# GpSimd's low parts of weight pieces, written in two operations of half the rows instead of one

## The chip, the cores and the metric

The kernel runs on one core of one Trainium2 chip. The core has five engines with a queue of instructions each: TensorE (PE in the profile, with its weight loads as PEld), VectorE (DVE), ScalarE (ACT), GpSimd (POOL) and SyncE (SP), which here only issues DMAs. Every queue is worked off in its order, and an instruction waits for semaphores that other engines raise. The metric is the device time of one execution in microseconds (us), shorter is better.

## What is computed

Two layers of a token backbone over 256 latent tokens and 256 context tokens of width 1024. A layer is a normalised and modulated input, one wide input projection, three mixing branches (latent attention, a long convolution, differential attention), their merge by sigmoid gates, an output projection, and a squared-ReLU MLP of width 4096. Cut to what matters here, the large products with weights:

```python
p  = h @ w_in                              # 1024 -> 5024, latent and context tokens
m  = g_a*(ya @ w_br_a) + g_b*(yb @ w_br_b) + g_c*(yc @ w_br_c)
y  = m @ w_out
x  = x + g_m * y
x  = x + g_f * (square(relu(h2 @ w_fc1)) @ w_fc2)   # 1024 -> 4096 -> 1024
```

All of it is float32. In the second layer only the 256 latent tokens go on after the attention's keys and values.

## The kernel before

**Weights in two parts.** TensorE multiplies float32 data in a format of fewer bits, fp32r. To keep the accuracy, each operand is split into a high part (the value cast to fp32r) and a low part (the value minus its high part), and `mm3` (line 265) makes each product of three matmuls: high by high (L270), low activations by high weights (L271 where the weight stands first) and high activations by low weights (L272). The profile's names tell which is which: `whi` and `wlo` are the parts of the weight, `hhi` and `hlo` those of the activations.

**Pieces.** A weight arrives from HBM in blocks of 1 MB (`raw`, two buffers), and a block is cut into pieces (`Unit`) of 128 partitions by 1024 values. Of a piece, the cast to `whi` runs on ScalarE in most cases (L222), and then the subtraction that makes `wlo` runs on VectorE (157 pieces of L223) or on GpSimd (69 pieces of L223, 3 of L234 in `split_rows` and 2 of L245 in `split_into`: 74 in all). `whi` and `wlo` have three buffers each. A piece is split one piece ahead of its use (`LOOK`).

**Which engine.** `pick_lo` (line 209) takes GpSimd or VectorE for the low part by a default that the caller sets (`lo_eng`) and by single exceptions in the table `CHOICE`. A piece is 8 rows of 128 values (`split_cols`, `split_into`) or 4 rows of 256 (`split_rows`) on each partition; a row k is what one group of three matmuls uses, so TensorE comes to a piece's rows one after the other.

**Order.** The steps are lists of Python functions that are woven by hand and then put in an order by the table `ORDER`; each engine's queue holds its instructions in the order in which the steps were written. The framework adds the waits: an instruction waits for the last writer of what it reads and for the last readers of what it overwrites.

**What stands around the GpSimd pieces.** VectorE has, beside its own low parts, the softmax of the attentions (`DVE L799` maximum out of PSUM, `L1226` and `L1230` which combine two probability tiles), the rotary step (`L787`, `L790`), the low parts of activations (`L480`, `L497`, `L277`), the merge (`L1324`, `L1328`) and parts of the MLP's squaring (`L1428`, `L1429`). GpSimd has also rotary products (`L789`), copies (`L1171`) and a few others. The wait of a new block's DMA (`SPq L254`) is for the last reader of the old block in that buffer, which is often a GpSimd low part.

Of the kernel before, what the change touches and what calls it, by code (L numbers as in the profile page):

```python
# [9 lines left out]
F32 = mybir.dt.float32  # L10
F32R = mybir.dt.float32r
AF = mybir.ActivationFunctionType
ALU = mybir.AluOpType
# [110 lines left out]
def backbone_kernel(ctx: ExitStack, tc: tile.TileContext, t, out):  # L124
# [9 lines left out]
    PE, ACT, DVE, POOL, SP = nc.tensor, nc.scalar, nc.vector, nc.gpsimd, nc.sync  # L134
# [64 lines left out]
    def pick(key, default):  # L199
        return CHOICE.get(key, default)  # L200
# [4 lines left out]
    def cp(key, default="A"):  # L205

        return {"A": ACT.copy, "D": DVE.tensor_copy, "P": POOL.tensor_copy}[pick(key, default)]

    def pick_lo(u, eng):
        return ENG[pick(f"lo{u.id}", "P" if eng is POOL else "D")]  # L210

    def split_cols(lo_col, own=None):
        eng = lo_eng["e"]

        def f(raw, u):
            if own:
                u.hi, u.lo = [S[own].tile([128, KT, 128], F32R, name=f"{own}{p}{lo_col}") for p in "hl"]
            else:
                u.hi = ring.tile([128, KT, 128], F32R, tag="whi", name="whi", bufs=UNIT_BUFS)
                u.lo = ring.tile([128, KT, 128], F32R, tag="wlo", name="wlo", bufs=UNIT_BUFS)  # L220
            src = raw[:, :, lo_col:lo_col + 128]
            cp(f"hi{u.id}")(u.hi, src)  # L222
            pick_lo(u, eng).tensor_tensor(out=u.lo, in0=src, in1=u.hi.bitcast(F32), op=ALU.subtract)  # L223
        return f

    def split_rows(kt0):
        eng = lo_eng["e"]

        def f(raw, u):
            u.hi = ring.tile([128, 4, 256], F32R, tag="whi", name="whi", bufs=UNIT_BUFS)  # L230
            u.lo = ring.tile([128, 4, 256], F32R, tag="wlo", name="wlo", bufs=UNIT_BUFS)
            src = raw[:, kt0:kt0 + 4, :]
            cp(f"hi{u.id}")(u.hi, src)
            pick_lo(u, eng).tensor_tensor(out=u.lo, in0=src, in1=u.hi.bitcast(F32), op=ALU.subtract)  # L234
        return f

    def split_into(lo_col, keep, c0):

        eng = lo_eng["e"]

        def f(raw, u):
            u.hi, u.lo = [b[:, :, c0:c0 + 128] for b in keep()]
            src = raw[:, :, lo_col:lo_col + 128]
            cp(f"hi{u.id}")(u.hi, src)
            pick_lo(u, eng).tensor_tensor(out=u.lo, in0=src, in1=u.hi.bitcast(F32), op=ALU.subtract)  # L245
        return f

    def rawtile(shape):
# [9 lines left out]
    def gemm_units(blk):  # L258
        return [Unit(blk, split_cols(0)), Unit(blk, split_cols(128))]
# [592 lines left out]
    def mla(l, nt):  # L852
# [5 lines left out]
        uq_ = w_in_units(l, 0)  # L858
        b2 = col_blk(t["w_in"][l], 0, C_PKV, 192)
        ukv_ = [Unit(b2, split_cols(c, "kvw" if l else None)) for c in (0, 64)]  # L860

        def g_pq(i):
# [286 lines left out]
    def diff(l, nt):  # L1149
# [25 lines left out]
        for which, c0 in ((0, C_DQ), (1, C_DK)):  # L1175
            qks.append([Step(qk(which, ct), Unit(col_blk(t["w_in"][l], 0, c0 + 128 * ct, 128), split_cols(0)))
                        for ct in range(2)])
# [492 lines left out]
```

## Time and profile before

| | |
|---|---|
| three runs, median (lowest to highest) | 1349.06 us (1346.07 to 1350.47) |
| the profiled execution, its own time | 1347.23 us |
| its span, first to last instruction | 1345.2 us |
| mean granted clock of TensorE | 0.984 |
| busy: TensorE, weight loads | 1289.5 us (96%), 1082.9 us (81%) |
| busy: VectorE, ScalarE, GpSimd | 876.7 us (65%), 588.0 us (44%), 257.6 us (19%) |
| the chain that ended last: TensorE, VectorE, ScalarE, GpSimd | 81%, 10%, 3%, 0% |

The profiled execution is 2.0 us longer than its span, and 1.8 us shorter than the median. The rows of a timeline read: start in us, length in us, engine, line, operation, what it writes and reads, how many were merged, and in brackets how long the engine was idle before and who ended that. A line of the waits reads: who waited for whom, total us, times, longest. A matmul's length includes its pipeline; how fast TensorE goes is seen in the distance between starts.

### The profile page before, as it was taken

How to read it: one execution, taken by the hardware profiler on the slowest of the kernel's cores; microseconds unless marked ns; L12 is line 12 of the kernel's file. 1: busy time of each engine (PE TensorE's matmuls, PEld its weight loads, DVE VectorE, ACT ScalarE, POOL GpSimd, SP SyncE). 2: the span in 40 equal slices, each digit the busy share in tenths (PEclk: the TensorE clock that was granted, in tenths of full speed). 3: DMA queues.
4: the chain of work that ended last, by engine and by line, in shares of the span. 5: the costliest groups of instructions: out<-in, count | busy, mean ns of one | idle time of the engine just before them, and what ended most of it. 6: DMA issues, size and time to landing. Idle time of an engine off the chain costs nothing.

```text
span 1345.2 us, 19813 instructions
## 1 busy us (share of the span) xinstructions
PE 1289.5 (96%) x7934; PEld 1082.9 (81%) x7934; DVE 876.7 (65%) x1406; ACT 588.0 (44%) x1034; POOL 257.6 (19%) x173
## 2 busy tenths in 40 slices
PE   4999999899999999999999999998998999999997
PEld 3576776567888898787787877996887999999997
DVE  4776736865244568986684775587667568976565
ACT  4454542564222344332332332364646654655343
POOL 2212131310001101120100112022234343230100
PEclk8899999999999999999999999998999999999999
DMA  9643243442233334654564553332133455455652
GB/s 267 176 147 112 79 125 105 148 152 70 91 102 98 109 100 128 216 188 162 168 200 128 170 160 115 111 103 78 49 97 99 127 164 162 157 188 183 191 186 94
DMA packets 159789, 185.20 MB, mean 138 GB/s; under 512 B 4880, under 2 KB 149233, under 8 KB 157650
## 3 DMA queue, kind: packets, MB, share of 16 engines
q1 hardware_dynamic: 158162, 182.27, 43.2%
q0 software_dynamic: 928, 1.54, 0.4%
q8 instruction: 62, 1.02, 0.3%
q14 instruction: 29, 0.24, 0.1%
q10 hardware_dynamic: 608, 0.14, 0.0%
HBM read 182.88 MB, written 1.05 MB: 137 GB/s over the span
## 4 chain that ended last, share of the span: by engine, by line
PE 81%; DVE 10%; ACT 3%; DMA 2%; issue 2%; POOL 0%; SPq 0%; ACTq 0%; DVEq 0%; POOLq 0%
PE g L270 15%; PE g L271 15%; PE g L272 14%; PE s L270 9%; PE s L272 9%; PE s L271 9%; PE o L839 2%; PE t L826 2%; PE mod L338 1%; DVE d L1168 1%; DVE hlo L480 1%; DVE wlo L223 1%; DMA mq<-in_w_mod_dram 1%; ACT whi L222 1%; ACT t L156 1%
## 5 line engine op out<-in xcount | busy, mean ns | idle before, releaser
L222 ACT CAST whi<-raw 128x1024 fp32r<-128x1024 f32 x203 | 212.7, 1049 | 443.3 <-PE g L271 215.7
L270 PE MATMUL g<-hhi,whi 128*128 128x512 f32 (+2 forms) x1040 | 355.3, 342 | 5.5 <-ACT ge L1297 1.6
L272 PE MATMUL g<-hhi,wlo 128*128 128x512 f32 (+2 forms) x1040 | 353.4, 340 | 0.5 <-DVE wlo L223 0.5
L271 PE MATMUL g<-hlo,whi 128*128 128x512 f32 (+2 forms) x1040 | 353.2, 340 | 0.2
L223 POOL TENSOR_TENSOR wlo<-raw,whi 128x1024 fp32r<-128x1024 f32 x69 | 174.2, 2526 | 637.5 <-ACT whi L222 503.8
L223 DVE TENSOR_TENSOR wlo<-raw,whi 128x1024 fp32r<-128x1024 f32 x157 | 194.2, 1238 | 146.2 <-ACT whi L222 138.7
L270 PEld LDWEIGHTS g<-hhi,whi 128*128 128x128 f32 x1040 | 196.4, 189 | 37.5 <-issue 7.0
L271 PEld LDWEIGHTS g<-hlo,whi 128*128 128x128 f32 x1040 | 197.0, 189 | 23.5 <-issue 0.8
L272 PEld LDWEIGHTS g<-hhi,wlo 128*128 128x128 f32 x1040 | 197.1, 190 | 23.2 <-DVE wlo L223 0.9
L374 DVE SCALAR_TENSOR_TENSOR macc<-modr,spad,macc 128x1024 f32<-128x1024 f32 x84 | 112.2, 1365 | 16.0 <-DMA modr<-in_w_mod_dram 15.0
L1350 DVE SCALAR_TENSOR_TENSOR x<-s,modT,x 128x256 f32<-128x256 f32 x95 | 43.4, 480 | 72.6 <-PE s L272 72.5
L272 PE MATMUL s<-hid0h,wlo 128*128 128x512 f32 (+1 forms) x256 | 87.0, 340 | 0.0
L271 PE MATMUL s<-hid0l,whi 128*128 128x512 f32 (+1 forms) x256 | 86.7, 339 | 0.0
L270 PE MATMUL s<-hid0h,whi 128*128 128x512 f32 (+1 forms) x256 | 86.6, 338 | 0.0
L272 PE MATMUL s<-hid1h,wlo 128*128 128x256 f32 (+1 forms) x224 | 72.7, 325 | 0.0
L270 PE MATMUL s<-hid1h,whi 128*128 128x256 f32 (+1 forms) x224 | 72.6, 324 | 0.0
L271 PE MATMUL s<-hid1l,whi 128*128 128x256 f32 (+1 forms) x224 | 72.2, 323 | 0.0
L156 ACT ACTIVATE t<-s,sm 128x512 f32<-128x512 f32 (+1 forms) x91 | 55.4, 612 | 36.6 <-DVE sm L799 35.9
L799 DVE TENSOR_REDUCE sm<-s 128x1 f32<-128x512 f32 (+1 forms) x75 | 51.4, 688 | 26.5 <-PE s L272 19.5
L270 PEld LDWEIGHTS s<-hid0h,whi 128*128 128x128 f32 x256 | 48.4, 189 | 7.3 <-ACT whi L222 0.8
L271 PEld LDWEIGHTS s<-hid0l,whi 128*128 128x128 f32 x256 | 48.0, 187 | 5.8
L272 PEld LDWEIGHTS s<-hid0h,wlo 128*128 128x128 f32 x256 | 48.1, 188 | 5.7
(467 smaller groups left out, 2433.7 us busy)
## 6 DMA issues: line engine op xcount, KB each, us to landing
raw<-in_w_fc_dram SPq DMA_DIRECT2D x64, 1024.0 KB, 5.4
raw<-in_w_in_dram SPq DMA_DIRECT2D x34, 1024.0 KB, 5.3
modr<-in_w_mod_dram SPq DMA_DIRECT2D x48, 512.0 KB, 4.3
raw<-in_w_mod_dram SPq DMA_DIRECT2D x16, 1024.0 KB, 5.0
mq<-in_w_mod_dram SPq DMA_DIRECT2D x16, 512.0 KB, 7.9
raw<-in_w_out_dram SPq DMA_DIRECT2D x8, 1024.0 KB, 5.1
raw<-in_w_in_dram SPq DMA_DIRECT2D x8, 512.0 KB, 3.9
raw<-in_w_br_a_dram SPq DMA_DIRECT2D x8, 512.0 KB, 3.4
```

The lines of the kernel that those rows point to most:

```text
L156: ins = ACT.activation(out=out, in_=in_, func=func, **kw).ins
L222: cp(f"hi{u.id}")(u.hi, src)
L223: pick_lo(u, eng).tensor_tensor(out=u.lo, in0=src, in1=u.hi.bitcast(F32), op=ALU.subtract)
L270: PE.matmul(ps, lhsT=ah, rhs=bh, start=first and i == 0, stop=False)
L271: PE.matmul(ps, lhsT=ah, rhs=bl, start=False, stop=False)
L272: PE.matmul(ps, lhsT=al, rhs=bh, start=False, stop=last and i == n - 1)
L338: PE.matmul(box["ps"][32 * j:32 * j + 32, :], lhsT=spad[:, kt, :], rhs=raw[:, 512 * j:512 * (j + 1)], start=kt == 0, stop=kt == KT - 1)
L374: DVE.scalar_tensor_tensor(out=a, in0=raw, scalar=sv, in1=a, op0=ALU.mult, op1=ALU.add)
L799: DVE.tensor_reduce(out=sm[:, c0:c0 + nseg], in_=ps.rearrange("p (s k) -> p s k", s=nseg), axis=AX.X, op=ALU.max, negate=True)
L826: PE.transpose(pt[:, j * 128:(j + 1) * 128], p[:, j * 128:(j + 1) * 128], ident)
L839: PE.matmul(o[64 * i:64 * i + 64, u * 128:(u + 1) * 128], lhsT=vals(k, i), rhs=pts[i][:, k * 128:(k + 1) * 128], start=k == 0, stop=k == 3)
L1350: DVE.scalar_tensor_tensor(out=x[:, n, c], in0=ps[:, c], scalar=modT[l][:, goff + n, s:s + 1], in1=x[:, n, c], op0=ALU.mult, op1=ALU.add)
```

## The change

A new function `lo_of` takes the place of the subtraction in the three split functions. If the piece's low part is VectorE's, it is made as before, in one operation. If it is GpSimd's, the rows are cut in two: the first operation writes rows 0 to 3 (of 8) or 0 and 1 (of 4), the second the rest. Choice of engines, tables, buffers and all other steps are the same.

```diff
+    def lo_of(u, src, eng):
+
+        e = pick_lo(u, eng)
+        n = src.shape[1]
+        w = n // 2 if e is POOL else n
+        for a in range(0, n, w):
+            e.tensor_tensor(out=u.lo[:, a:a + w], in0=src[:, a:a + w], in1=u.hi[:, a:a + w].bitcast(F32), op=ALU.subtract)
+
     def split_cols(lo_col, own=None):
...
             cp(f"hi{u.id}")(u.hi, src)
-            pick_lo(u, eng).tensor_tensor(out=u.lo, in0=src, in1=u.hi.bitcast(F32), op=ALU.subtract)
+            lo_of(u, src, eng)
```

The last two lines stand alike in `split_rows` and `split_into`. All later lines move down by 8: the low part's L223, L234 and L245 become L218, the matmuls' L270 to L272 become L278 to L280.

On GpSimd's queue, in the first layer's differential attention (`d` are its queries and keys, `ysp` the convolution's spectrum, `t` scratch), before:

```order
L1171 COPY d_1896<-d_1896 32x512 x3
L1123 TENSOR_TENSOR ysp_1914<-ysp_1914,t 128x512
L223 TENSOR_TENSOR wlo<-raw,whi 128x1024 x3
L1171 COPY d_2233<-d_2233 32x512
L789 TENSOR_TENSOR t<-t,rs 128x256
L1171 COPY d_2233<-d_2233 32x512
```

and now:

```order
L1179 COPY d_1905<-d_1905 32x512 x3
L1131 TENSOR_TENSOR ysp_1923<-ysp_1923,t 128x512
L218 TENSOR_TENSOR wlo<-raw,whi 128x512 x6
L1179 COPY d_2243<-d_2243 32x512
L797 TENSOR_TENSOR t<-t,rs 128x256
L1179 COPY d_2243<-d_2243 32x512
```

Three operations have become six of half the size at the same place; the 74 pieces give 148 operations, and nothing else on this queue is added or moved. On the other queues no instruction is added, taken away or moved, but waits are. On TensorE's queue, in the second layer's merge (`yah` and `ybh` are high parts of two branches' outputs, the piece's rows 0 to 3 go with `yah`, rows 4 and 5 with `ybh`), before:

```order
L272 MATMUL s<-yah,wlo 128x256
L270 MATMUL s<-yah,whi 128x256
L271 MATMUL s<-yal,whi 128x256
L272 MATMUL s<-yah,wlo 128x256
L270 MATMUL s<-ybh,whi 128x256 [waits DVE_49]
L271 MATMUL s<-ybl,whi 128x256
L272 MATMUL s<-ybh,wlo 128x256
```

and now:

```order
L280 MATMUL s<-yah,wlo 128x256
L278 MATMUL s<-yah,whi 128x256
L279 MATMUL s<-yal,whi 128x256
L280 MATMUL s<-yah,wlo 128x256
L278 MATMUL s<-ybh,whi 128x256 [waits DVE_49]
L279 MATMUL s<-ybl,whi 128x256
L280 MATMUL s<-ybh,wlo 128x256 [waits Pool_49]
```

Beside the wait for GpSimd at the piece's first low matmul, which it had before, the first matmul with row 4 waits too, for the second operation. 69 such waits come on TensorE. DMAs of new blocks and casts to `whi` that waited for GpSimd now wait for the second of the two operations.

## Rows read from the trace of the kernel before

**Rows 1.** Waits of TensorE: total us, times, longest
```profile
PE t L826 <- DVE t L1230: 7.0, 4, 3.8
```

**Rows 2.** GpSimd's groups by form: count | busy us, mean ns | idle before
```profile
L223 POOL TENSOR_TENSOR wlo<-raw,whi 128x1024 fp32r<-128x1024 f32 x69 | 174.2, 2526 | 637.5 <-ACT whi L222 503.8 <-DVE whi L222 98.7 <-DVE x L1350 20.4
L1123 POOL TENSOR_TENSOR ysp<-ysp,t 128x512 f32<-128x512 f32 x1 | 1.3, 1263 | 15.0 <-DVE t L1122 15.0
```

**Rows 3.** Timeline, GpSimd and VectorE, first layer's differential attention
```profile
236.05 2.40 POOL L223 TENSOR_TENSOR wlo<-raw,whi 128x1024 fp32r<-128x1024 f32 x1 [8.31 <-ACT whi L222]
236.06 0.68 DVE L799 TENSOR_REDUCE sm<-s 128x1 f32<-128x512 f32 x1
236.66 2.34 DVE L1230 SCALAR_TENSOR_TENSOR t<-t,sm 128x512 f32<-128x512 f32 x1
...
240.13 4.69 POOL L223 TENSOR_TENSOR wlo<-raw,whi 128x1024 fp32r<-128x1024 f32 x2 [1.68 <-ACT whi L222]
240.27 2.27 DVE L1226 SCALAR_TENSOR_TENSOR sm<-ss,nlam,sm 128x1 f32<-128x1 f32 x1
...
242.57 2.79 DVE L1230 SCALAR_TENSOR_TENSOR t<-t,sm 128x512 f32<-128x512 f32 x1
...
247.28 0.74 DVE L1230 SCALAR_TENSOR_TENSOR t<-t,sm 128x512 f32<-128x512 f32 x1
```

**Rows 4.** Timeline, TensorE's two waits in the same stretch
```profile
239.05 0.33 PE L826 MATMUL t<-ident,t 128*128 128x128 f32 x1 [0.43 <-DVE t L1230]
...
245.42 0.33 PE L826 MATMUL t<-ident,t 128*128 128x128 f32 x1 [3.85 <-DVE t L1230]
```

**Rows 5.** Busy time by window (PE, PEld, DVE, ACT, POOL), granted clock, DMA
```profile
246.50:249.80 3.30, 3.30 (x10) 2.56 (x9) 3.30 (x11) 1.98 (x5) 0.00 (x0) 0.50 0.67 276
```

**Rows 6.** Timeline, two GpSimd low parts back to back, second layer's MLP
```profile
1193.58 2.41 POOL L223 TENSOR_TENSOR wlo<-raw,whi 128x1024 fp32r<-128x1024 f32 x1 [9.15 <-ACT whi L222]
...
1194.27 2.01 DVE L1428 TENSOR_TENSOR t<-t 128x256 f32<-128x256 f32 x1 [3.05 <-ACT hid1h L1427]
1196.31 2.52 DVE L1429 TENSOR_TENSOR hid1l<-t,hid1h 128x256 fp32r<-128x256 f32 x1
...
1195.95 2.60 POOL L223 TENSOR_TENSOR wlo<-raw,whi 128x1024 fp32r<-128x1024 f32 x1
```

**Rows 7.** Timeline, second layer's rotary step before its differential attention
```profile
987.03 2.40 POOL L234 TENSOR_TENSOR wlo<-raw,whi 128x1024 fp32r<-128x1024 f32 x1 [1.36 <-ACT whi L233]
987.14 2.58 DVE L790 TENSOR_TENSOR g<-t 128x256 f32<-128x256 f32 x1
...
993.23 0.38 PE L270 MATMUL g<-whi,hhi 128*128 128x256 f32 x1 [1.25 <-DVE d L1168]
```

**Rows 8.** Timeline, second layer's start: two low parts of activations
```profile
888.70 2.41 DVE L480 SCALAR_TENSOR_TENSOR hlo<-t,modT,hhi 128x256 fp32r<-128x256 f32 x2
...
890.76 0.39 PE L271 MATMUL o<-hlo,kvwh 128*128 128x256 f32 x1 [1.43 <-DVE hlo L480]
```

**Rows 9.** Timeline, second layer's merge
```profile
1090.05 1.96 DVE L277 TENSOR_TENSOR ml<-ge,mh 128x256 fp32r<-128x256 f32 x1
...
1095.46 0.39 PE L270 MATMUL s<-yah,whi 128*128 128x256 f32 x1 [1.11 <-DVE ge L1324]
...
1125.09 0.38 PE L270 MATMUL g<-mh,whi 128*128 128x256 f32 x1 [1.45 <-ACT mh L276]
```

**Rows 10.** Timeline, GpSimd and TensorE, second layer's differential attention
```profile
1016.67 0.73 POOL L789 TENSOR_TENSOR t<-t,rs 128x256 f32<-128x256 f32 x1
...
1021.74 0.66 PE L826 MATMUL t<-ident,t 128*128 128x128 f32 x4 [1.92 <-DVE t L1230]
```

**Rows 11.** Timeline, a GpSimd low part, TensorE's matmuls with rows 0 and 4
```profile
1112.15 2.47 POOL L223 TENSOR_TENSOR wlo<-raw,whi 128x1024 fp32r<-128x1024 f32 x1 [4.62 <-DVE whi L222]
...
1115.57 0.28 PE L272 MATMUL s<-yah,wlo 128*128 128x256 f32 x1
...
1116.99 0.29 PE L272 MATMUL s<-ybh,wlo 128*128 128x256 f32 x1
```

More of the change, by code (lines that the diff above doesn't have):

```diff
@@ L233, in f @@
             cp(f"hi{u.id}")(u.hi, src)
-            pick_lo(u, eng).tensor_tensor(out=u.lo, in0=src, in1=u.hi.bitcast(F32), op=ALU.subtract)
+            lo_of(u, src, eng)
         return f
@@ L244, in f @@
             cp(f"hi{u.id}")(u.hi, src)
-            pick_lo(u, eng).tensor_tensor(out=u.lo, in0=src, in1=u.hi.bitcast(F32), op=ALU.subtract)
+            lo_of(u, src, eng)
         return f
```

## The prediction, made before the changed kernel was run

> **What bounds the kernel now.** I read the waits of TensorE first. TensorE is busy for 96% of the span, so what can be won lies in its idle time or in its clock. Its list shows two things. It has no wait for a low part that GpSimd makes. And the largest item behind the start is VectorE's L1230, 7.0 us in four waits [rows 1]. So I asked why L1230 is late, in the timeline of both engines [rows 3]. The second and third L1230 there do the same work on the same shape, and so does the first: 0.74 us where GpSimd is idle, 2.34 and 2.79 us beside a GpSimd low part. The first began at 236.66, while GpSimd worked from 236.05 to 238.45, and ended at 239.00, 0.55 us after GpSimd. L1226, a tiny operation, took 2.27 us in the same way. L799, which reads PSUM, took its 0.68 us beside the same GpSimd operation. So a VectorE operation with both inputs in SBUF stands still until the GpSimd operation in flight is over, and TensorE sees that: 0.43 and 3.85 us idle for these two L1230 [rows 4]. After the 3.85 us its granted clock stood at 0.50, the 1.2 GHz level, for a stretch of 3.3 us with TensorE busy throughout [rows 5].
>
> The price of a GpSimd low part is therefore the time for which it holds VectorE, and the change cuts that piece of time in two.
>
> **The change part by part.**
>
> *1. Two operations for one.* A subtraction of 1024 values takes 2.40 us undisturbed [rows 3], 2.53 us in the mean of 69 [rows 2]. Of half the size there is one row, the L1123 of 1.26 us [rows 2], with two inputs of SBUF as well. Back to back, the second of two GpSimd operations starts 0.04 us before the first ends (1193.58 + 2.41 = 1195.99 against 1195.95, [rows 6]). So a pair takes 2 x 1.26 - 0.04 = 2.48 us: 0.1 us more each, 74 x 0.1 = 7 us on GpSimd, which is idle for 81% of the span. It lies beside TensorE's work, and what shows of it is in term 6.
>
> *2. TensorE's 69 waits more.* They cost nothing if the second half is there. The tightest case that I found is the piece that ends at 1114.62, whose first low matmul starts at 1115.57, 0.95 us later [rows 11]. The second half is due 12 matmuls after that, at 1116.99, and comes 0.1 us later than the whole did, plus what VectorE takes in between, 0.3 to 1.2 us: at 1115.9 at the latest, which leaves 1.1 us to spare. Zero, in the range up to 0.5 us. Here the cover is the piece that is split ahead; without it each unit would show the 0.1.
>
> *3. The pair of waits in the first layer's differential attention.* Now: GpSimd's first half ends at 236.05 + 1.26 = 237.31, so L1230 ends 0.55 us behind it, at 237.86 instead of 239.00, and the 0.43 us [rows 4] go. VectorE's queue is then 0.7 us or more ahead, and the next L1226 and L1230 can start around 239.7, before GpSimd's next piece at 240.13; then the 3.85 us go too. If VectorE isn't ahead, L1226 is held by the first half to 241.4, L1230 by the second to 242.6, and ends at 243.2 instead of 245.36: 2.2 us gained. Between 2.2 and 3.85 I take 3.3, nearer to the upper end, because the first L1230 is released with certainty, but something else (the following probabilities, which come 0.5 us too late for TensorE by the same reckoning) is late next. The stretch at half clock [rows 5] costs 3.3 / 2 = 1.65 us. It came right behind the 3.85 us in which TensorE stood; with most of that idle time gone, I expect it to go. Sum: 0.4 + 3.3 + 1.65 = 5.35, between 2.6 and 5.9.
>
> *4. The rotary step of the second layer.* L790 is held from 987.14 and ends at 989.72, 0.29 us after GpSimd [rows 7]. With halves: 987.03 + 1.26 + 0.29 = 988.58, 1.1 us earlier. What follows on ScalarE and VectorE up to TensorE's wait at 993.23 reads PSUM on one side and isn't held by the second half. 1.1 of the 1.25 us go.
>
> *5. Where two held operations follow each other.* Behind the first half one VectorE operation goes in, then the second half, and the second VectorE operation stands again. At the second layer's start two L480 in a row took 2.41 us [rows 8]: the first would be done 1.1 us sooner, the second at the same time as before, and TensorE needs the second three matmuls after the first. Its wait of 1.43 us is only cut in two: gain 0. In the merge [rows 9], L277 (1.96 us) is released 1.1 us earlier, but an L1328 behind it meets the second half, and the same happens before 1125.09: I take 0.4 us of each of the waits of 1.11 and 1.45 us. Together 0.8, between 0 and 2.
>
> *6. What gets later.* An operation of VectorE that today starts in the last half of GpSimd's piece waits 0.1 us longer, and so does what stands behind the piece on GpSimd's queue: L789 at 1016.67, which feeds a wait of TensorE of 1.92 us [rows 10]. About six such places lie on the way to a wait: 0.6 us. DMAs of new blocks wait for the second half, 0.1 to 0.7 us later; TensorE has no wait for a cast to `whi` in its list, so this is covered by the second buffer; without that cover it would be 0.1 us per block.
>
> Sum: 5.35 + 1.1 + 0.8 - 0.6 = 6.65 us of the profiled execution's 1347.23, so 1340.6. The profiled execution is 1.83 us below the median of the runs, and the changed kernel will be judged by its median: 1349.06 - 6.65 = **1342.4 us**. I expect the gaps of the other stretches, the MLPs above all, to stay: TensorE has no wait there that a held VectorE operation ends.
>
> **Does VectorE get in between the halves?** All of this rests on it. Since the next GpSimd operation starts before the one in front has ended, GpSimd could hold on. Rows 6 show the case: L1428 waits from 1194.27 through GpSimd's first piece, ends at 1196.28, 0.29 us after that piece's end, and the second GpSimd piece, already started, takes 2.60 instead of 2.40 us. L1429, next on VectorE, then stands until this second piece is over. In rows 3 the tiny L1226 too ended at 242.54, in the middle of the pair of 4.69 us. So they take turns. The Trainium skill (GPSIMD Engine Reference, Instruction dispatch) states a rule that speaks against the change: consecutive Pool instructions are no barrier, each of the eight cores starts the next as soon as its own share is done. By that rule alone the two halves would overlap and could be one uninterrupted hold, and the sum would be that of rival A, 1350. The overlap of 0.04 us agrees with the rule, the turn that VectorE gets at that border doesn't agree with an uninterrupted hold.
>
> **Rivals.**
>
> *A. The halves hold VectorE like one piece.* Then each held operation is released 0.1 us later instead of 1.1 us earlier. Some ten places lie before a wait: 1 us slower, 1350. For it: the 0.04 us overlap, and that both halves are ready in GpSimd's queue without a wait between. Against it: rows 6 and rows 3. Chance 0.12.
>
> *B. Taking turns gives little.* As in term 5, the second half catches the next operation in the attention too, TensorE's wait of 3.85 us becomes 1.7, and another stretch at half clock comes or stays. Then 2.6 + 0.5 - 0.6 = 2.5 us are gained, 1346.5. For it: L1226 and L1230 follow each other directly [rows 3]. Against it: VectorE gets ahead by the first release. Chance 0.22.
>
> *C. Slower, by TensorE's clock.* In the second layer's differential attention TensorE stands for 1.92 us before 1021.74 [rows 10] and the granted clock stays full. GpSimd's L789 behind a longer pair, and copies behind it, lengthen just these waits. If the clock falls there for a stretch as in rows 5, that is 1.65 us, and if it falls in two more places of the second layer where it now holds, 5 us, with the 5.35 us of term 3 not coming since another wait ends last there: 1354. It decides from the point at which three stretches fall and term 3 fails. For it: TensorE stands there too, and in rows 4 and 5 the clock did fall behind a stand. Against: the added delay is 0.1 us beside a wait of 1.92 us after which it didn't fall. Chance 0.06.
>
> That the change doesn't do what it says can be left out: the instruction order shows 148 operations of half the size.
>
> **How the numbers follow.** My forecast (term 3 in most of its size, 1338 to 1345) has 0.60. B (1345 to 1349) has 0.22, A (1349 to 1351) 0.12, C 0.06. The range reaches from 1338, where terms 3 and 5 come in full (5.9 + 1.1 + 2 + 1.4 for a second clock stretch avoided), to 1348.8 at the end of B, and leaves out A and C. A measurement of this kernel can tell about 0.3%, 4 us, from no change. Faster by more than that is 1345 and below: 0.60. Within: B and A, 0.33 with a little of C. Slower by more: 0.07.
>
> **What would show it.** The half operations: 148 on GpSimd, 1.2 to 1.3 us each where nothing holds them. Held L1230, L790, L277 at most 1.9 us instead of 2.3 to 2.8. TensorE's wait for L1230 down from 7.0 us to below 4, the one before 993.23 gone, and the granted clock full through 245 to 250. Two L480 still at 2.4 us together. If held operations still take 2.3 us and more, A is right; if L1230 is short and the time the same, look for a wait that has moved. What would make the prediction wrong is a different alignment of the engines at 236 to 246, on which 5 of the 6.65 us rest.

## The result, and the profile after

The changed kernel took 1334.91 us in the median of five runs (1330.72 to 1340.07), the kernel before 1348.47 (1346.07 to 1350.47): a ratio of 0.991, 95% interval 0.989 to 0.993, or 13.6 us. A second comparison of the same two gave 1337.47 and 1348.13 us, 0.992 (0.990 to 0.994), 10.7 us. The forecast was 6.65 us: right in its direction and in the mechanism, about half of the first figure and three fifths of the second. The profiled execution took 1338.25 us, 9.0 less than that of before; its span is 1336.5 us.

TensorE's waits after, those that answer to [rows 1], [rows 7], [rows 8] and [rows 9] (who waited for whom, total us, times, longest):

```profile
PE t L834 <- DVE t L1238: 4.8, 5, 1.9
...
PE g L278 <- DVE d L1176: 1.9, 4, 1.1
...
PE o L279 <- DVE hlo L488: 1.1, 2, 0.8
...
PE s L278 <- DVE ge L1332: 0.8, 1, 0.8
...
PE g L278 <- ACT mh L284: 0.5, 1, 0.5
```

All five are shorter than before (7.0, 2.8, 1.4, 1.1 and 1.4 us), and still none is for a low part of GpSimd. The timeline of the first layer's attention, which answers to [rows 3] and [rows 4]:

```profile
233.89 1.32 DVE L1234 SCALAR_TENSOR_TENSOR sm<-ss,nlam,sm 128x1 f32<-128x1 f32 x1
...
235.74 1.26 DVE L1238 SCALAR_TENSOR_TENSOR t<-t,sm 128x512 f32<-128x512 f32 x1
...
238.27 0.99 DVE L1234 SCALAR_TENSOR_TENSOR sm<-ss,nlam,sm 128x1 f32<-128x1 f32 x1
239.30 1.73 DVE L1238 SCALAR_TENSOR_TENSOR t<-t,sm 128x512 f32<-128x512 f32 x1
...
233.90 2.54 POOL L218 TENSOR_TENSOR wlo<-raw,whi 128x512 fp32r<-128x512 f32 x2 [8.20 <-ACT whi L230]
237.95 5.45 POOL L218 TENSOR_TENSOR wlo<-raw,whi 128x512 fp32r<-128x512 f32 x4 [1.50 <-PE t L834]
...
237.05 0.33 PE L834 MATMUL t<-ident,t 128*128 128x128 f32 x1 [0.47 <-DVE t L1238]
241.08 0.33 PE L834 MATMUL t<-ident,t 128*128 128x128 f32 x1 [1.49 <-DVE t L1238]
```

The held L1238 take 1.26 and 1.73 us instead of 2.34 and 2.79, the held L1234 1.32 and 0.99 instead of 2.27. Where VectorE gets its turns, GpSimd is the one that stands: four halves take 5.45 us here, against 2.54 for a pair that loses no turn. Over the whole kernel a half takes 1.42 us in the mean, so a pair costs GpSimd about 0.3 us more than the 2.53 us of a whole piece [rows 2] (GpSimd's group by form):

```profile
L218 POOL TENSOR_TENSOR wlo<-raw,whi 128x512 fp32r<-128x512 f32 x144 | 201.9, 1422 | 637.6 <-ACT whi L230 517.2 <-DVE whi L230 96.5 <-ACT whi L241 16.5
```

TensorE's wait of 3.85 us has become 1.49; that of 0.43 is still there, with 0.47, because the small L1234 started 0.01 us before GpSimd this time and was held before L1238 was.

The granted clock (windows; the columns as in [rows 5], the clock is the third number from the end):

```profile
241.50:244.80 3.30, 3.12 (x16) 2.10 (x15) 3.30 (x8) 1.53 (x5) 1.90 (x2) 1.00 0.22 32
1016.40:1019.70 3.30, 3.30 (x18) 3.30 (x17) 3.24 (x6) 1.86 (x4) 0.00 (x0) 0.50 0.07 7
1117.60:1121.00 3.40, 2.75 (x22) 2.55 (x23) 1.86 (x4) 1.74 (x3) 0.84 (x1) 1.00 0.82 283
```

It stays full behind the shortened wait in the attention, where it was 0.50 [rows 5], and behind the merge, where before it was 0.50 for 3.4 us from 1127.1. On the other side there is a stretch at half clock from 1016.4, behind the wait of 1.9 us of [rows 10], which hasn't changed, and the one from 921, 6.8 us before, is 10.2 us long.

The swap of the stretch behind the merge for one from 1016 need not be the change's doing. A second profile of the kernel before (it is among the experiments) has it too. The windows are of the kernel before in its first profile, then twice in its second:

```profile
1127.10:1130.50 3.40, 3.40 (x18) 3.40 (x18) 2.33 (x2) 1.23 (x3) 2.37 (x1) 0.50 0.00 0
```
```profile
1026.50:1029.90 3.40, 3.40 (x19) 3.40 (x18) 3.34 (x7) 1.86 (x4) 0.00 (x0) 0.50 0.10 10
1128.00:1136.00 8.00, 6.33 (x51) 6.14 (x52) 6.43 (x9) 4.01 (x7) 2.40 (x1) 1.00 0.37 123
```

The rotary step, the second layer's start and the merge, against [rows 7] to [rows 9] (timeline; start, length):

```profile
980.42 2.72 POOL L218 TENSOR_TENSOR wlo<-raw,whi 128x512 fp32r<-128x512 f32 x2 [1.21 <-ACT whi L241]
980.53 1.47 DVE L798 TENSOR_TENSOR g<-t 128x256 f32<-128x256 f32 x1
...
985.53 0.38 PE L278 MATMUL g<-whi,hhi 128*128 128x256 f32 x1 [0.17 <-DVE d L1176]
...
882.85 2.29 DVE L488 SCALAR_TENSOR_TENSOR hlo<-t,modT,hhi 128x256 fp32r<-128x256 f32 x2
...
883.78 0.39 PE L279 MATMUL o<-hlo,kvwh 128*128 128x256 f32 x1 [0.29 <-DVE hlo L488]
...
885.20 0.39 PE L279 MATMUL o<-hlo,kvwh 128*128 128x256 f32 x1 [0.80 <-DVE hlo L488]
...
1088.82 0.39 PE L278 MATMUL s<-yah,whi 128*128 128x256 f32 x1 [0.77 <-DVE ge L1332]
...
1117.52 0.38 PE L278 MATMUL g<-mh,whi 128*128 128x256 f32 x1 [0.51 <-ACT mh L284]
```

L798 is held for 1.47 us instead of 2.58 and TensorE's 1.25 us are 0.17. The two L488 take 2.29 us together, 2.41 before: one gets in between the halves, the second is caught by the second half, and one wait of 1.43 us has become two of 0.29 and 0.80.

Where the 8.7 us of span went, by the starts of the same matmuls in both traces (before minus after, worked out): 2.2 us until 210 us, 3.2 from there to 263, 0.5 to 867, 3.2 from 867 to 1147, and 0.4 lost behind that. The second and the fourth were forecast. Of the first, 2.9 us are there at 36 us already, before the first piece is cut, and nothing in the forecast speaks of it.

One sentence ahead of the prediction has to be put right: that nothing else on GpSimd's queue moved. At two places an operation that stood behind a piece now stands between its halves; one is at 911 us, the other is L797 here:

```profile
1006.59 1.29 POOL L218 TENSOR_TENSOR wlo<-raw,whi 128x512 fp32r<-128x512 f32 x1 [7.68 <-ACT whi L230]
...
1007.85 0.74 POOL L797 TENSOR_TENSOR t<-t,rs 128x256 f32<-128x256 f32 x1
...
1008.54 1.29 POOL L218 TENSOR_TENSOR wlo<-raw,whi 128x512 fp32r<-128x512 f32 x1
...
1008.62 1.50 DVE L798 TENSOR_TENSOR g<-t 128x256 f32<-128x256 f32 x1 [1.19 <-POOL t L797]
```

L797 is done 1.1 us sooner, but L798, which needs it, is caught by the second half: from the piece's start to the end of L798 it took 3.55 us before (1014.31 to 1017.86) and takes 3.53 now.

### The profile page after: what moved, and what is told of

Its sections match the earlier page's. It is cut to its first block, busy times and chain, and to the rows that moved or that the text cites. A ratio compares the mean times of both kernels' runs of the same rounds, so it can differ in the third digit from the quotient of the medians.

```text
span 1336.5 us, 19918 instructions
## 1 busy us (share of the span) xinstructions
PE 1286.9 (96%) x7934; PEld 1080.9 (81%) x7934; DVE 868.0 (65%) x1406; ACT 587.7 (44%) x1034; POOL 278.9 (21%) x247
## 4 chain that ended last, share of the span: by engine, by line
PE 71%; DVE 8%; ACT 2%; DMA 2%; issue 1%; POOL 0%; DVEq 0%; ACTq 0%; SPq 0%; POOLq 0%
PE g L278 13%; PE g L279 13%; PE g L280 13%; PE s L278 8%; PE s L280 8%; PE s L279 8%; DMA raw<-in_w_fc_dram 1%; PE o L847 1%; PE t L834 1%; DVE d L1176 1%; DVE hlo L488 1%; DVE wlo L218 1%; ACT whi L230 1%; DVE t L485 1%; PE mod L346 1%
## 5 line engine op out<-in xcount | busy, mean ns | idle before, releaser
L278 PE MATMUL g<-hhi,whi 128*128 128x512 f32 (+2 forms) x1040 | 355.0, 342 | 5.6 <-ACT ge L1305 1.6
L280 PE MATMUL g<-hhi,wlo 128*128 128x512 f32 (+2 forms) x1040 | 353.0, 340 | 0.5 <-DVE wlo L218 0.5
L218 POOL TENSOR_TENSOR wlo<-raw,whi 128x512 fp32r<-128x512 f32 x144 | 201.9, 1422 | 637.6 <-ACT whi L230 517.2
L218 DVE TENSOR_TENSOR wlo<-raw,whi 128x1024 fp32r<-128x1024 f32 x158 | 197.1, 1249 | 154.1 <-ACT whi L230 147.0
L278 PEld LDWEIGHTS g<-hhi,whi 128*128 128x128 f32 x1040 | 196.1, 189 | 37.5 <-issue 7.0
L280 PEld LDWEIGHTS g<-hhi,wlo 128*128 128x128 f32 x1040 | 196.9, 189 | 23.2 <-DVE wlo L218 0.9
L280 PE MATMUL s<-hid0h,wlo 128*128 128x512 f32 (+1 forms) x256 | 87.0, 340 | 0.0
L278 PE MATMUL s<-hid0h,whi 128*128 128x512 f32 (+1 forms) x256 | 86.6, 338 | 0.0
L280 PE MATMUL s<-hid1h,wlo 128*128 128x256 f32 (+1 forms) x224 | 72.7, 325 | 0.0
L278 PE MATMUL s<-hid1h,whi 128*128 128x256 f32 (+1 forms) x224 | 72.6, 324 | 0.0
L278 PEld LDWEIGHTS s<-hid0h,whi 128*128 128x128 f32 x256 | 48.4, 189 | 7.3 <-ACT whi L230 0.8
L280 PEld LDWEIGHTS s<-hid0h,wlo 128*128 128x128 f32 x256 | 48.1, 188 | 5.7
```

Of the source, the lines that this page charges most:

```text
L218: e.tensor_tensor(out=u.lo[:, a:a + w], in0=src[:, a:a + w], in1=u.hi[:, a:a + w].bitcast(F32), op=ALU.subtract)
L278: PE.matmul(ps, lhsT=ah, rhs=bh, start=first and i == 0, stop=False)
L280: PE.matmul(ps, lhsT=al, rhs=bh, start=False, stop=last and i == n - 1)
```

## Experiments

Theory 1 is that of the prediction: the length of one GpSimd operation sets how long VectorE is held, and the waits named there shrink. Its rivals are named in the expectations. Each run was timed against the kernel before on the same chip; the median of that was between 1347.2 and 1348.1 us.

**The changed kernel once more.** No edit.

> The changed kernel once more, to see the granted clock of every run of it and of the kernel before. If the gain beyond the 6.65 us of the forecast is fewer stretches at half clock in all of its executions (theory 1), the runs of the changed kernel show a mean clock of 0.988 or more against 0.984 or less before, and their time falls as the clock rises; the median is 10 to 15 us below the kernel before. If it came from the start of the kernel (2 us less in the profile until 20 us) and from chance (theory 2), the clocks of the two kernels overlap and the gain of the medians shrinks to 6 to 9 us.

1337.47 us, 0.992. The five clocks were 0.985 to 0.988, those of 23 runs of the kernel before 0.981 to 0.987: so both theories are partly met, the clock is higher by some 0.002 but overlaps. In the runs of the kernel before the time falls by 0.8 us for each 0.001 of mean clock (a straight line through the 23 runs; 0.5 to 0.9 us in the three other sets of runs of that kernel), so that is 1.8 us of 10.7 by this estimate. The start is faster again, by 4.4 us at 210.

**Cut at some places only.** The condition in `lo_of` is the only difference; the third is the rest of both.

```diff
-        w = n // 2 if e is POOL else n
+        w = n // 2 if u.id in (15, 18, 19) else n
```
```diff
-        w = n // 2 if e is POOL else n
+        w = n // 2 if e is POOL and 128 <= u.id <= 180 else n
```
```diff
-        w = n // 2 if e is POOL else n
+        w = n // 2 if e is POOL and u.id not in (15, 18, 19) and not 128 <= u.id <= 180 else n
```

> Two operations only in the three pieces at 236 to 245 us, in the first layer's differential attention; the other 71 pieces as before. Theory 1 (the time for which a GpSimd operation holds VectorE): TensorE's wait of 3.85 us becomes about 1.5 us and the half clock behind it goes, 1.5 us more: 4 us faster than before, 0.997. Rival (the gain is spread over all pieces, since rows 0 to 3 of a low part and the buffers come earlier everywhere): 3 of 74 pieces give under 1 us.

> Two operations only in the 27 or so pieces from the second layer's start to its merge (880 to 1143 us before). Theory 1: 1.1 us before the second layer's L480, 1.1 in the rotary step, 1.3 in the merge, and two stretches at half clock behind these waits (891 and 1127 us) of 1.5 us each gone, one new one possible: 4 to 7 us faster, 0.995 to 0.997. Rival as for the first layer's pieces: 27 of 74, about 5 us, without change in those three waits.

> Two operations in all pieces but those of the two kernels before it: 44 pieces of the start, the branches of the first layer and both MLPs. Theory 1: no wait of TensorE there is ended by a held VectorE operation, so the time is that of the kernel before within 1 us, 1.000; up to 2 us less if the first 20 us are part of it. Rival (gain spread over all pieces): 8 us faster.

Three pieces of 74 give 1342.78 us, 0.9957 (0.9941 to 0.9974): 5.35 us. In the profile the wait of 3.85 us is 1.62 and the clock behind it full. The pieces of the second layer give 1347.24 us, 0.9973 (0.9952 to 0.9995): 0.9 us in the medians, where 4 to 7 were expected, with a wide spread: four of twelve runs took 1337 to 1341 us at a clock of 0.989 to 0.992, the others 1343 to 1351 at 0.981 to 0.985. The profiled one is of the latter: the waits are shortened as in the changed kernel, but the clock falls behind the merge as before, and for 6.8 us from 1020.8. What tells the fast four from the others isn't settled. The 43 pieces that are left give 1347.99 us, 1.0002 (0.9988 to 1.0016): nothing. So a gain that is spread over all pieces is out; it lies where a held VectorE operation ends a wait. But 5.35 and 0.9 make 6.2 us, and the whole gave 10.7 on this chip. All three kernels also lack the faster start: TensorE reaches the matmul that is at 205.2 us before (L348, which is L356 where `lo_of` stands in the kernel) at 205.3, 207.0 and 207.9 us in them, at 203.0 and 200.8 in the two profiles of the changed kernel.

**Both places together.**

```diff
-        w = n // 2 if e is POOL else n
+        w = n // 2 if e is POOL and (u.id in (15, 18, 19) or 128 <= u.id <= 180) else n
```

> Two operations in the three pieces of the first layer's attention and in those from the second layer's start to its merge together, 30 or so in all, the other 44 as before. Theory 1 with the start as a cause of its own: the two gains add up (2.6 and 2.4 us at equal clock, more where stretches at half clock go): 1341 to 1343 us, start as before (223 to 229 GB/s). Rival (no cause at the start; the cut in the 44 others matters after all when these 30 are cut): 1341 to 1343 too but with 250 GB/s at the start, or 1337 us.

1337.79 us, 0.9918 (0.9902 to 0.9935): a gain of 9.8 us, where 1341 to 1343 us were expected. The start is as before (229 GB/s, L348 at 204.5 us), so it isn't that. The mean clock is 0.989 against 0.985 in the kernel before, 3 us by the 0.8 us for each 0.001. So the two parts together give 3.6 us more than their gains alone (6.2 us), and nothing here shows why. Timeline of its attention, then its clock windows:

```profile
235.54 2.99 POOL L218 TENSOR_TENSOR wlo<-raw,whi 128x512 fp32r<-128x512 f32 x2 [8.28 <-ACT whi L230]
...
236.18 1.20 DVE L1238 SCALAR_TENSOR_TENSOR t<-t,sm 128x512 f32<-128x512 f32 x1
...
239.13 0.21 DVE L1234 SCALAR_TENSOR_TENSOR sm<-ss,nlam,sm 128x1 f32<-128x1 f32 x1
...
239.38 0.75 DVE L1238 SCALAR_TENSOR_TENSOR t<-t,sm 128x512 f32<-128x512 f32 x1
...
239.75 2.76 POOL L218 TENSOR_TENSOR wlo<-raw,whi 128x512 fp32r<-128x512 f32 x2 [1.22 <-ACT whi L230]
```
```profile
241.50:244.80 3.30, 3.30 (x19) 2.39 (x18) 3.30 (x8) 2.39 (x6) 3.30 (x3) 1.00 0.37 154
884.00:888.00 4.00, 3.20 (x26) 3.00 (x26) 4.00 (x6) 2.43 (x5) 0.86 (x1) 1.00 0.00 0
1117.60:1121.00 3.40, 2.66 (x21) 2.47 (x22) 1.86 (x4) 1.78 (x4) 0.67 (x1) 1.00 0.86 292
```

Here VectorE is ahead: the second L1234 and L1238 run before GpSimd's next piece at 239.75, unheld, and both waits of [rows 4] are gone, as the prediction had it (5.0 us from 210 to 263 by the matmuls' starts). The changed kernel's second profile and the next two kernels show the same (4.7 to 5.0 us), as do the two kernels with the cut and a moved tile further below (4.8 and 4.9). In the changed kernel's first profile and in that of the three pieces alone it is 3.2 and 3.1. So term 3 has two outcomes. In both of the latter the first L1234 and GpSimd's first half start within 0.01 us of each other and L1234 is held; in the four others with halves it starts 0.07 to 0.35 us ahead and isn't. The clock is full also behind L488 and behind the merge, where before it fell for 3.4 us each.

**The halves in the other order.**

```diff
-        for a in range(0, n, w):
+        for a in reversed(range(0, n, w)):
```

> As the changed kernel, but of each pair the rows 4 to 7 are written first and rows 0 to 3, which TensorE needs first, last. Theory 1 (what counts is for how long one GpSimd operation holds VectorE): nothing changes against the changed kernel, 1334 to 1338 us, no wait of TensorE for GpSimd's low parts, and TensorE's waits for L1238, L488 and L1176 as there. Rival (the first rows' low part is ready 1.2 us earlier, and that is the gain): the gain is lost, 1348 us. The start: if the 2 to 4 us that both profiles of the changed kernel save in the first 50 us belong to a program of this size, they are here too; if they are chance, they may be missing.

1337.16 us, 0.9921 (0.9907 to 0.9935), no wait for a low part. When the first rows are ready doesn't matter for the time; theory 1 holds.

**Four operations.**

```diff
-        w = n // 2 if e is POOL else n
+        w = n // 4 if e is POOL else n
```

> Each low part of GpSimd in four operations of two rows, 296 in all. An operation of 256 values takes 0.73 us in the trace of the kernel before, so a held VectorE operation is released after 0.73 us at most instead of 1.26, and a piece takes 2.8 us in place of 2.5. Theory 1: TensorE's waits in the first layer's attention together fall from about 2.0 to about 1 us, the one before L488 from 1.1 to 0.5: 1.5 us faster than the changed kernel, 1333 to 1337 us. Rival (VectorE's turn at each border delays GpSimd and so what waits for it; four borders cost more than they give): 1 to 4 us slower than the changed kernel, with new waits for GpSimd's L797 or for low parts.

1337.18 us, 0.9918 (0.9904 to 0.9931), equal to the reversed halves on the same chip: the 1.5 us expected beyond the halves didn't come. Its waits, two rows of its attention, and a row of ScalarE in the second layer's MLP (timelines):

```profile
PE t L834 <- DVE t L1238: 2.3, 2, 1.5
...
PE g L278 <- ACT t L1434: 1.7, 2, 1.2
...
PE s L280 <- POOL wlo L218: 0.5, 2, 0.3
...
PE o L279 <- DVE hlo L488: 0.3, 1, 0.3
```
```profile
234.24 3.30 POOL L218 TENSOR_TENSOR wlo<-raw,whi 128x256 fp32r<-128x256 f32 x4 [8.16 <-PE s L1221]
...
234.27 0.71 DVE L1234 SCALAR_TENSOR_TENSOR sm<-ss,nlam,sm 128x1 f32<-128x1 f32 x1
```
```profile
1181.20 1.04 ACT L230 CAST whi<-raw 128x1024 fp32r<-128x1024 f32 x1 [3.79 <-DMA raw<-in_w_fc_dram]
```

The mechanism goes on: the held L1234 takes 0.71 us, and TensorE's wait for L488 is 0.3 instead of 1.1. But a piece now takes up to 3.3 us, and TensorE waits for GpSimd's low parts for the first time, 0.5 us. By the starts of the matmuls quarters gain 6.7 us from 867 to 1147 us, against 3.2 and 3.0 in the two profiles of the changed kernel, and lose 3.1 behind it, in the second layer's MLP. Most of that loss is in the 1.7 us that TensorE waits for ScalarE's L1434, which stands behind a cast that waits for its block's DMA.

**The start.** The kernel before for a second profile; with 74 tiny GpSimd writes behind its last low part, first to an unused tile, then to a table that is no longer read; the same writes on VectorE; 58 of them.

```diff
+    pad = const.tile([128, 8], F32, name="pad")
...
             fin["ps"] = [[bank(tag) for tag in ("t", "g")] for i in range(2)]
+            for _ in range(74):
+                POOL.memset(pad, 0.0)
```
```diff
             fin["ps"] = [[bank(tag) for tag in ("t", "g")] for i in range(2)]
+            for _ in range(74):
+                POOL.memset(rc[:, 0:8], 0.0)
```

> The kernel before, unchanged, for a second profile of it. Theory 1 expects the three waits as in the first profile (3.85 us before 245, 1.43 before 891, 1.25 before 993) and 1348 us. The start, if it varies by chance: the matmul that follows the first modulation (205.2 us in the first profile, 203.0 and 200.8 in the two of the changed kernel, 205.3 to 207.9 in the three partial ones) lies anywhere from 201 to 208 us; if it belongs to the program, within 0.5 us of 205.2.

> The kernel before with 74 very small GpSimd writes of zeros to an unused tile behind its last low part, so that the program is as long as the changed one, and no low part is cut in two. If the 2 to 4 us at the start belong to the longer program (where its instructions lie, how they are loaded): the start is 2 to 4 us shorter and the time 1344 to 1346 us. If they are chance or belong to the cut: 1348 us, the start between 204 and 208 us.

> The kernel before with 74 very small GpSimd writes of zeros behind its last low part, this time into a table that is not read any more, so that no tile moves in SBUF. In the profiles so far the DMAs move 223 to 229 GB/s in the first 20 us in five programs with up to 44 GpSimd operations more than before, and 250 to 264 GB/s in five with 74 or more. If the program's length decides it: 250 GB/s or more, the start 2 to 4 us shorter, and no other gain: 1343 to 1346 us, less than the 1338 us of the kernel with the unused tile. If it is the cut itself or chance: 223 to 229 GB/s and 1348 us.

> The kernel before with the 74 small writes on VectorE instead of GpSimd, at the same place. If the length of the whole program decides the DMAs at the start: 250 GB/s or more in the first 20 us, the start 2 to 4 us shorter. If GpSimd's own part of the program does: 223 to 229 GB/s and the start as before. The end may be 1 to 4 us longer by the writes themselves.

> The kernel before with 58 small GpSimd writes instead of 74. The partial kernel with 44 GpSimd operations more had 223 GB/s at the start, the one with 74 more 262. A steady effect of length gives a rate in between, 235 to 250 GB/s; a step gives one of the two, 223 to 229 or 250 to 264.

The kernel before, run once more, took 1346.26 us, 0.9989 (0.9977 to 1.0002). In its second profile the three waits are as in the first (3.89, 1.37 and 1.25 us), and it reached L348 at 206.9 us, 1.7 us later than in the first: one profile's start says no more than that. With the 74 writes to the old table it is reached at 200.9, and the runs take 1344.73 us, 0.9977 (0.9961 to 0.9994): 2.9 us gained (0.8 to 5.3 by the interval) by writes that nobody needs. On VectorE they give nothing (204.3 us, 1348.18, 1.0002), and 58 on GpSimd give 201.7 and 1344.3, 0.9976 (0.9963 to 0.9989). What is faster are the DMAs in the first 20 us (page of that window; packets, MB and mean rate), in the order before, after, 74 writes on GpSimd, 74 on VectorE:

```profile
DMA packets 6468, 4.57 MB, mean 229 GB/s; under 512 B 1165, under 2 KB 5927, under 8 KB 6468
```
```profile
DMA packets 6647, 5.00 MB, mean 250 GB/s; under 512 B 1178, under 2 KB 6011, under 8 KB 6647
```
```profile
DMA packets 6714, 5.25 MB, mean 262 GB/s; under 512 B 1184, under 2 KB 6017, under 8 KB 6714
```
```profile
DMA packets 6365, 4.42 MB, mean 221 GB/s; under 512 B 1156, under 2 KB 5857, under 8 KB 6365
```

Over all 18 profiles of this study: the eight with 74 or more additional GpSimd operations moved 250 to 264 GB/s and reached L348 after 202.4 us in the mean (200.8 to 203.9); the nine with 43 or fewer moved 221 to 229 and took 205.6 (204.3 to 207.9); the one with 58 moved 244. The two groups don't overlap. So 3.2 us of the change's gain, in the mean of the profiles, have nothing to do with cutting a piece: they come with a longer GpSimd program, here with cuts and with writes alike. By which way the program's length reaches the DMAs of the start isn't settled: GpSimd's own issues stand at the same times (1.50 us before, 1.49 after, for the first), and no profile shows where programs and tensors lie in memory.

The first of these kernels (74 writes to the unused tile) took 1337.93 us, 9.3 less than before, much more than its start explains. That is another cause.

**The place of the tiles.** The unused tile shifts all tiles allocated after it by 32 bytes. The tile with one write, in the kernel before, in the changed one and in that with quarters; and a tile of 64 bytes.

```diff
+    pad = const.tile([128, 8], F32, name="pad")
...
+            POOL.memset(pad, 0.0)
```

> The kernel before with the unused tile of 32 bytes and one write to it, so that all tiles allocated later lie 32 bytes further on, and no more instructions. In the kernel with the tile and 74 writes a stretch of 1250 matmuls without a gap took 259.7 us, in all others 262.6. If the place of the tiles sets the matmuls' pace: 259.7 us in that stretch, 5 us gained over the whole, 1343 us, start as before (223 to 229 GB/s). If the pace came from the longer program: 262.6 us and 1348 us.

> The kernel before with an unused tile of 64 bytes instead of 32. The stretch of 1250 matmuls without a gap took 262.6 us before and 259.7 with 32 bytes. If any other place than the old one helps: 259.7 again, 1341 to 1343 us. If the place modulo 64 bytes counts: 262.6 us, 1348 us.

> The changed kernel with the unused tile of 32 bytes and one write to it. If the three causes (shorter holds, faster DMAs at the start, pace of the matmuls) add up: 5 us below the changed kernel, 1330 to 1333 us. If they stand in for each other, 1335 to 1338 us.

> Low parts of GpSimd in four operations, and the unused tile of 32 bytes. Quarters alone gave 1337.2 us, halves 1337.2 to 1337.5 on the same chips, halves with the tile 1334.1. If the parts add up: 1330 to 1333 us. If quarters give nothing beyond halves: 1334 us.

The tile alone gives 1341.36 us, 0.9946 (0.9931 to 0.9962), with the slow start (226 GB/s). The same stretch of the first layer's MLP, in which TensorE doesn't wait at all, in windows of TensorE (busy us, matmuls, clock) of the kernel before and of this one:

```profile
604.60:868.00 263.40, 263.40 (x1258) 1.00 0.48 151
```
```profile
601.90:862.00 260.10, 260.10 (x1255) 1.00 0.48 153
```

209.4 ns per matmul against 207.3, at the same full clock. From its matmul number 3100 to number 4350 this stretch takes 262.6 us in every kernel without the tile and 259.7 or 259.8 in the four with 32 bytes. With 64 bytes it is 262.4, and still the whole is as fast, 1340.65 us, 0.9947 (0.9931 to 0.9962): there the end, from 1200 us on, is 2.3 us shorter (1.5 with 32 bytes). Both profiles, with the tile, one write and no cut, also gain 1.8 us from 210 to 263 us: the second of the small operations (L1226 before) starts 0.06 to 0.08 us ahead of GpSimd and isn't held. TensorE's wait of 3.85 us is 1.6 there, and the half clock behind it stays. Neither expectation fits: the place counts, but not in one stretch alone, and not by 64 bytes. The change moves no tile, and its pace is that of before (262.6 us), so this has no part in its gain.

The causes add up in part. Halves with the tile take 1334.11 us, 0.9899 (0.988 to 0.9918): 13.5 us gained, between the two expectations, where 10.1 to 10.7 for the halves and 6.2 for the tile would make 16.3 to 16.9. Quarters with the tile take 1329.01 us (1327.20 to 1332.86), 0.9865 (0.9842 to 0.9888), 18.4 us below the kernel before, where 10.1 and 6.2 would make 16.3, and the fastest here. The clocks of its four runs are 0.986 to 0.992, which helps.

## Why the prediction was right or wrong

*What bounds the kernel and whether VectorE gets in between* was right. The held operations of [rows 3], [rows 7] and [rows 9] became shorter by 1.0 to 1.3 us, about the length of half a piece, and L1234 and L1238 shorter again with quarters. The Trainium skill (SBUF — State Buffer, section "SBUF: two separate sides") calls the port pair of VectorE and GpSimd an exclusive lock that is held for the whole instruction, also where VectorE has two SBUF inputs. The rows agree: held operations of VectorE took 2.34, 1.26 and 0.71 us beside GpSimd operations of 2.40, 1.29 and 0.74. Rival A (halves hold like one) is out. That section of the Trainium skill doesn't say whose turn it is between two queued GpSimd operations; here it was VectorE's.

*Terms 1 and 2* were right in what they add to the sum: 2.54 us for a pair that loses no turn against 2.48, and no wait of TensorE for the second half. Term 1's 7 us on GpSimd were too few: it is busy for 278.9 us instead of 257.6, 21 us more, since a half that VectorE gets ahead of takes up to 1.7 us.

*Term 3* (5.35 us) held in four profiles of kernels without the tile (4.7 to 5.0 from 210 to 263 us) and was 3.2 in the one recorded with the result, where VectorE wasn't ahead: the case that its lower end of 2.2 us describes. That "the first L1230 is released with certainty" was too much, since L1234 in front of it can be held instead. TensorE's waits for it are 4.8 us there, not below 4, and 2.7 where VectorE is ahead. Its clock part is borne out: the half clock behind these waits stands in all ten profiles without the cut there and in none of the eight with it. That the shorter wait alone ends it isn't shown, since in the two profiles with the tile, one write and no cut the wait is 1.6 us and the half clock stays.

*Term 4* was right: 1.08 us of 1.25.

*Term 5* (0.8 us) was too small: 0.34 us at L488, 0.34 and 0.93 in the merge, 1.6 us. It left out most of the clock. Two stretches at half clock, behind 891 us and behind 1127, of which I had put one into the range and none into the sum, went in the changed kernel (1.2 and 1.6 us, the change of the matmuls' starts there less that of the waits). Over all profiles that is only in part the cut's doing. The one behind 891 is absent in six of eight profiles with the cut there and in two of ten without. The one behind 1127 is absent in seven of eight, but also in six of ten without the cut, the kernel before's second profile among them. In the first profile the new one at 1016.4 (1.5 us) and the longer one at 921 (0.9 us) take most of both back.

*Term 6* (0.6 us lost) was of the right size for another reason: from 1147 us on 0.4 us are lost in the first profile and 1.5 in the second, in waits of the MLP, while at L797, which was my example, nothing is. In the second, 1.2 us of them are waits for ScalarE's L1434 behind a cast that waits for its block's DMA, as with quarters: the DMAs of new blocks, which term 6 took as covered. Whether the DMA is later by the halves or TensorE is there sooner isn't told apart.

*The sum.* Without the start, the profiles give 6.5 and 7.0 us for the changed kernel and 6.5 for the reversed one: what the six terms speak of came to about what they said. One profile of before is a weak base, though, since its second profile differs from it by 0.3 to 0.6 us in each of these stretches. Against the mean of the five profiles that have neither a cut nor the tile, the mean of the three with halves in all pieces gains 4.7 us from 210 to 263, 0.5 to 867 and 2.6 to 1147, and loses 0.6 behind that: 7.2 us.

The step that failed is the frame around the terms, that TensorE's time outside these places stays: the start was put at nothing. It gave 3.2 us more in the mean of the profiles, from a cause in which cutting the pieces has no part. 7.2 + 3.2 = 10.4 us, against 10.7 in the second comparison and 10.1 for the reversed kernel. That this agrees so well may be luck, because the kernel with the cut at both places gained 9.8 us without the faster start, which this sum doesn't explain.

The first comparison, 13.6, has five runs with clocks from 0.982 to 0.994, whose time falls with the clock from 1340 to 1331 us; the mean clock of the kernels with the cut in all pieces and no tile is 0.987 to 0.988, that of the kernel before 0.984 to 0.986, 2 us by the 0.8 us for each 0.001, of which term 3 holds 1.65. What sets it from run to run is open, and so are the 3.2 us that the first comparison has beyond the 10.4.

*Rival C* did happen at its place (half clock from 1016.4), but the clock falls somewhere between 1004 and 1027 us in 15 of the 18 profiles, that of the kernel before's second among them, and it was one stretch, not three. Seven of the ten profiles without the cut in that layer have it, so it doesn't need the change. The range ended at 1338.0 us (its own sum, 5.9 + 1.1 + 2 + 1.4 = 10.4 us, ends at 1338.7): it carried my own terms to their ends and nothing for what no row of before shows.

## What to carry to other kernels

If VectorE's operations on two SBUF operands are slow beside GpSimd, make the GpSimd operation shorter: it is its single length that holds VectorE, and a cut cost GpSimd 0.1 us per piece alone and 0.3 with VectorE's turns in between. Cutting on is not free: quarters were no faster than halves here, and 5.1 us faster only beside the moved tiles. Cut first where a held operation ends a wait of the engine that bounds the kernel; 31 of the 74 pieces, cut alone, gained 9.8 us, and the other 43 nothing. And before a difference of 10 us in 1350 is given to a change, run a kernel in which the change is without effect but the program is as long and the tiles lie as far along.

## What was not expected of the hardware

With 74 GpSimd operations that nobody needs at the end of the program, the DMAs move 257 and 262 GB/s in its first 20 us (250 to 264 in all programs with 74 or more of them), where they move 221 to 229 with 43 or fewer; 74 on VectorE change nothing (221 GB/s). And 32 bytes in front of the tiles shorten a stretch of 1250 matmuls from 262.6 to 259.7 us at the same clock. Neither is explained here.

The granted clock also falls at places that move from one profile of the same kernel to the next: the two of the kernel before have the half clock behind the merge and from 1026.5 us, each in one only. A stretch that is there before and gone after isn't shown to be an effect of a change by one profile of each.
